# A two-layer encoder trunk: six small moves in the order of a split-precision matmul kernel

## The chip, the cores and the metric

The kernel runs on one core of one Trainium2 chip. The metric is device time in microseconds, from one launch of the program. Three timed runs of the kernel before gave 2052.45, 2053.11 and 2056.63 us; the median is 2053.11 us.

## The reference, cut to what matters

`x` has 256 rows of 2048 numbers in float32. Layer A is a forgetting attention and a feed-forward, then keys and values are made once, then layer B is a chunked attention with its own query projection and a second feed-forward. Everything is computed in float32.

```python
def sq_relu_mlp(h, g, w1, w2):
    a = jax.nn.relu(rms_norm(h, g) @ w1)      # 2048 -> 8192
    return (a * a) @ w2                       # 8192 -> 2048

def reference(x, ...):
    u = rms_norm(h, a_norm_g[l]); proj = u @ a_w_in[l]        # q, k, v and a forget gate per head
    logf = jax.nn.log_sigmoid(fz + a_b_f[l])
    o = forgetting_attention(q, k, v, logf)
    h = h + o.reshape(B, S, D) @ a_w_out[l]
    h = h + sq_relu_mlp(h, mlp_norm_g[0], mlp_w1[0], mlp_w2[0])    # first feed-forward
    kv = rms_norm(h, kv_norm_g) @ kv_w
    q = rms_norm(h, b_norm_g[l]) @ b_w_q[l]                        # query projection
    o = chunked_relbias_attention(q, k_sh, v_sh, b_rel[l])
    h = h + o.reshape(B, S, D) @ b_w_out[l]
    h = h + sq_relu_mlp(h, mlp_norm_g[1], mlp_w1[1], mlp_w2[1])    # second feed-forward
```

## The kernel before, in words

**Units and splits.** All weight matmuls run in a rounded float32 format (fp32r), three passes for one product. A weight *unit* is 128x1024. ScalarE makes `hi`, the rounded copy (L323), VectorE makes `lo = raw - hi` (L324), and TensorE runs hi x x_hi (L592), hi x x_lo (L594) and lo x x_hi (L596), 12 matmuls of 128x512 a unit (or 6, below). There are three `hi` and three `lo` buffers, so the hi of a unit can only be written when the L594 of the unit three before has read its buffer, and its lo when the L596 of that unit has. A split is written into the program two units ahead of its use (`AHEAD`, `fetch`, `top_up`).

**Pairs.** Two blocks of 512 output columns, made for both blocks of 128 rows, form a *pair*, and part of its inner dimension is done by a scheme with seven products in place of eight. A pair has four weight quarters ("11", "12", "21", "22") and four sums of them: T3 = 22 - 12, T2 = T3 + 11, T1 = 12 - 11, T4 = 21 - T2 up to signs. The seven products run in the order 11, T3, T2, T1, then those called 4 (of 21), 5 (of T4, "the fourth sum") and 6 (of 22, "the seventh product"). Products T3, T2, T1 and 22 multiply sums of the activations, called S or Sh, which `sums` makes: four VectorE subtractions (L395 to L398), two ScalarE roundings (L402), two VectorE remainders (L405). In the feed-forward pairs quarters and sums are 2048 columns wide, so each product has two halves of 6 matmuls, and each half is a unit of its own for the ring of three buffers. The rest of the inner dimension goes in *own units*, a4 to a7 and b4 to b7, 12 matmuls each; a is the first block of columns, b the second. The accumulators of a and b are tied by a few instructions on the accumulators: L1007, L1012, L1017 after the second and third product, and L1024 (called V), which adds the saved product `p7`, stands behind the pair's first own unit of a, and must be done ahead of the seventh product and of b's own units. T4 is made by a DMA issued from GpSimd that adds the quarter 21 onto T2's tile in place (`put`, L979).

**Order.** Each engine does its instructions in the order in which the program writes them; a wait at one instruction holds up all behind it on that engine. The table `ORD` holds the order of a pair's own units and last three products (each "F" takes the next of them, in the order that `FO` gives), and the rest of a pair's plan is fixed: four products with the previous pair's last own units b5, b6, b7 between them. Side work stands in a queue of slots, `fill`; `run_fill` takes one slot at each product or own unit. Tables of slot numbers (`T`, `T0H`, `T0K`) say at how many slots after a tile is finished each step of its side work runs.

**Feed-forward.** Each feed-forward runs pairs of the first matrix (hidden tiles) and of the second in turn. The first pair of the first matrix is called "early", the next "second"; then comes "deep0", the first pair of the second matrix, which reads the hidden tiles made by them. A finished hidden tile goes through `turn_hidden`: two VectorE transposes (L440) into `z`; a turn of rows and columns, either through DRAM (L450 writes, L456 reads four pieces) or by sixteen small DMAs that SyncE and GpSimd issue in turn (`hop`, L466); then `take`: Relu on ScalarE (L1045), Square rounded to hi (L1050), Square (L1052), the remainder lo on VectorE (L1056), and for two of a chunk's four tiles the eight instructions of `sums`. The numbers n = 0 to 3 count a chunk's tiles.

**Elsewhere.** The forget gates of layer A (`gates`, `logs`, L876 to L882) run as side work at about 50 to 60 us of the span, while query, key and value products run. The "query" pair, of layer B's projection, follows the first feed-forward's last pair, at about 1035 us.

Of the kernel before, what the change touches and what calls it, by code (L numbers as in the profile page):

```python
# [12 lines left out]
ALU = mybir.AluOpType  # L13
# [18 lines left out]
    "ATB": ((11, 12, 14, 18, 9), (9, 13, 15, 17, 11), (9, 12, 15, 17, 10), (7, 10, 12, 12, 10)),  # L32
# [16 lines left out]
    "OFK": (9, 9, 4, 8, 8, 4),  # L49
# [50 lines left out]
def trunk(ctx: ExitStack, tc: tile.TileContext, xT, xr, gs, hg, bf, wgate, w_in, w_oa, w1a, w1fa, w1sa, w2fa, w2sa,  # L100
# [706 lines left out]
    def begin(u):  # L807
        if u == 0:
            load(2, S, SY)
            S.activation(first, mhalf, AF.Square)  # L810
            SY.dma_start(raw_x[0][:, UA:], xT[:, UA:GH, :])
            load(2)
            load_x(1)
        elif u in (2, 4):
            load_x(u // 2 + 1)
        for j in range(UA):
            x.append(split_x(raw_x[u // 2][:, u % 2 * UA + j], u * UA + j, 0))
        for i, at in enumerate(TABLES["RI"][:3]):
            if u == at:
                rows_in(i)  # L820
        if u >= TABLES["RI"][3]:
            enter(u - TABLES["RI"][3])
# [26 lines left out]
    def gates(x, st):  # L849
# [22 lines left out]
        def logs():  # L872
# [5 lines left out]
            V.tensor_tensor(u, box[0][:H, :T], z, op=ALU.add)  # L878
            V.tensor_tensor(u, u, w, op=ALU.add)
            V.tensor_tensor(u, u, st.R[:H, :], op=ALU.mult)  # L880
            V.tensor_scalar(u, u, bfb, None, op0=ALU.add)
# [15 lines left out]
        def turn_c():  # L897
            pc = ps_o.tile([P, 512], F32, name="pt", tag="po")
            ct["cq"] = const.tile([P, NB, H], F32, name="cq")
            for b in range(NB):  # L900
# [3 lines left out]
        step, spread = steps(logs), steps(st.spread)  # L904
        return [[clear], [], [parts], [lambda: products(range(8))], [lambda: products(range(8, KT))], [spread], [spread],
                [step], [step], [step], [step], [turn_c]]
# [74 lines left out]
    def prepare(p, d):  # L981
# [5 lines left out]
        for name, at in zip(("12", "22", "21", "11", "T3", "T1"), p.units):  # L987
            if d == at and p.deep and name == "T3":
                make(p, "T3", 0)
            elif d == at:  # L990
                (bring if name[0] != "T" else put if p.adds and name == "T1" else make)(p, name)

    def run(plan, open_pair, masks=None, follow=None):
        starts = [i for i, it in enumerate(plan) if it[1:] == (2, 0)] + ([len(plan)] if follow else [])
        for i, (p, q, u) in enumerate(plan):
            hi, lo = ready.popleft()[:2] if q > 1 and ready and not p.deep else fetch()
            if p.ps is None:
# [3 lines left out]
            if q > 1:  # L1001
                assert u != 6 or "V" in p.has, "22 early"
                assert u != 3 or "V" not in p.has, "T1 late"
                form_products(p.ps, hi, lo, p.x, p.fs, u, q == 3, p)
                if u == 1 and q == 2 + p.wide:
                    p.t["P7"] = wk.tile([P, 512], F32, name="p7", tag="wk")
# [13 lines left out]
            else:  # L1020
                assert not p.fast or q == 0 or "V" in p.has, "b early"
                products(p.ps[q], hi, lo, p.x, u, not units and not ready, p.fast)
                if p.fast and (q, u) == (0, p.own):
                    V.tensor_tensor(p.ps[1][1], p.ps[1][0], p.t["P7"], op=ALU.add)  # L1024
                    p.has.add("V")
                for _ in range(1 if masks is None else masks[i]):
# [12 lines left out]
    def mlp(plan, x, Sx, st, last, more=None):  # L1039
# [28 lines left out]
        def turn_hidden(c, n):  # L1068
            zt = []

            def f(b, ps):
# [3 lines left out]
                if b == NB - 1:  # L1075
# [3 lines left out]
                    items = [[] for _ in range(max(at) + 1)]  # L1079
                    for i, d in zip([i for i in at if i >= 0], way + [step] * (len(at) - 2)):  # L1080
                        items[i].append(d)
# [18 lines left out]

    halves_of, owner = {}, {}

# [268 lines left out]
```

## Time and profile before

| | us |
|---|---|
| timed runs, median (lowest, highest) | 2053.11 (2052.45, 2056.63) |
| the profiled execution, its own time | 2058.22 |
| span of that execution, first to last instruction | 2056.4 |
| TensorE matmul busy | 2046.3 |
| VectorE busy | 1784.8 (87%) |
| ScalarE busy | 1403.9 (68%) |
| GpSimd busy | 247.0 (12%) |
| mean granted TensorE clock | 0.999 |
| bytes moved by DMA | 557.78 MB, mean 271 GB/s |

The profile's times are microseconds from the start of the span. A row of the timeline gives the start, the busy time (of all the instructions of a row with a count), engine, source line, operation, tiles and shapes, the count, and in brackets the idle time of that engine just before it and what ended it. PE is the matmul part of TensorE, PEld its weight loads, DVE is VectorE, ACT is ScalarE, POOL is GpSimd, SP is SyncE. Busy times of matmuls overlap their followers a little; the distance between starts is the pace.

### The profile page before, as it was taken

What the parts mean: (1) busy time and instruction counts of PE and PEld (TensorE: products, weight loads), DVE (VectorE), ACT (ScalarE), POOL (GpSimd) and SP (SyncE); (2) the same over time, 40 slices, a digit from 0 to 9 for tenths busy, and PEclk for the clock granted to TensorE, in tenths of its full rate; (3) what the DMA queues carried; (4) which work ended last, traced back from release to release, by engine and by line L of the source; (5) the groups of instructions that cost most, each with busy time, mean ns of one, the idle gap of its engine ahead of it and who ended that gap; (6) DMA issues with size and microseconds to landing.
All of it is one profiled execution on the core that took longest, in us unless ns stands there. A gap on an engine that the chain in (4) does not pass through costs nothing.

```text
span 2056.4 us, 27097 instructions
## 1 busy us (share of the span) xinstructions
PE 2046.3 (100%) x9062; PEld 1688.9 (82%) x9062; DVE 1784.8 (87%) x2065; ACT 1403.9 (68%) x1805; POOL 247.0 (12%) x351
## 2 busy tenths in 40 slices
PE   9999999999999999999999999999999999999999
PEld 8888888878888888888878888888788887888887
DVE  7788898898898899899988778888988997988996
ACT  7766666677677677677778666666766775776764
POOL 1111110021111102101012111001101111111020
PEclk9999999999999999999999999999999999999999
DMA  8898898998888898898889988888989888888984
GB/s 321 262 300 267 268 276 249 298 278 270 283 264 279 271 292 276 254 285 280 244 243 310 279 260 274 251 274 279 288 285 273 272 270 265 257 287 257 300 259 149
DMA packets 175310, 557.78 MB, mean 271 GB/s; under 512 B 40625, under 2 KB 69185, under 8 KB 152641
## 3 DMA queue, kind: packets, MB, share of 16 engines
q1 hardware_dynamic: 154112, 464.99, 64.1%
q0 software_dynamic: 20768, 90.75, 22.6%
q8 instruction: 71, 1.16, 0.2%
q14 instruction: 71, 0.57, 0.1%
q10 hardware_dynamic: 288, 0.30, 0.0%
HBM read 516.07 MB, written 27.29 MB: 264 GB/s over the span
## 4 chain that ended last, share of the span: by engine, by line
PE 92%; DMA 3%; DVE 3%; issue 1%; ACT 1%; SPq 0%; POOL 0%; DVEq 0%; ACTq 0%; POOLq 0%
PE acc L596 22%; PE acc L592 22%; PE acc L594 22%; PE s L596 8%; PE s L592 8%; PE s L594 8%; DVE lo L324 1%; DMA wT<-in_w1fa 1%; DMA wT<-in_w1fb 1%; PE po L729 1%; PE po L766 1%; DMA w<-in_w2fb 1%; DMA q<-turn 0%; DMA R<-turn 0%; PE po L728 0%
## 5 line engine op out<-in xcount | busy, mean ns | idle before, releaser
L324 DVE TENSOR_TENSOR lo<-raw,hi 128x1024 fp32r<-128x1024 f32 (+1 forms) x409 | 494.0, 1212 | 82.2 <-ACT hi L323 78.0
L323 ACT ACTIVATE hi<-raw 128x1024 fp32r<-128x1024 f32 (+1 forms) x409 | 429.2, 1054 | 191.1 <-PE acc L594 127.3
L592 PE MATMUL acc<-hi,act 128*128 128x512 f32 x1774 | 496.4, 393 | 0.9 <-DVE acc L1024 0.6
L596 PE MATMUL acc<-lo,act 128*128 128x512 f32 x1774 | 491.2, 390 | 1.0 <-DVE lo L324 0.8
L594 PE MATMUL acc<-hi,act 128*128 128x512 f32 x1774 | 490.7, 389 | 0.1
L596 PEld LDWEIGHTS acc<-lo,act 128*128 128x128 f32 x1774 | 332.1, 188 | 73.5 <-DVE lo L324 4.7
L594 PEld LDWEIGHTS acc<-hi,act 128*128 128x128 f32 x1774 | 332.8, 188 | 70.4 <-DVE act L421 0.5
L592 PEld LDWEIGHTS acc<-hi,act 128*128 128x128 f32 x1774 | 331.4, 188 | 70.5 <-ACT hi L323 1.8
L323 ACT ACTIVATE hi<-w 128x1024 fp32r<-128x1024 f32 x254 | 266.7, 1058 | 125.8 <-PE acc L594 82.2
L324 DVE TENSOR_TENSOR lo<-wT,hi 128x1024 fp32r<-128x1024 f32 x220 | 267.2, 1221 | 68.6 <-ACT hi L323 64.7
L324 DVE TENSOR_TENSOR lo<-w,hi 128x1024 fp32r<-128x1024 f32 x254 | 305.4, 1217 | 17.2 <-ACT hi L323 15.0
L323 ACT ACTIVATE hi<-wT 128x1024 fp32r<-128x1024 f32 x220 | 231.9, 1060 | 106.3 <-PE acc L594 58.2
L592 PE MATMUL s<-hi,act 128*128 128x512 f32 x530 | 146.4, 391 | 0.0
L596 PE MATMUL s<-lo,act 128*128 128x512 f32 x530 | 145.2, 389 | 0.0
L594 PE MATMUL s<-hi,act 128*128 128x512 f32 x530 | 144.8, 388 | 0.0
L466 POOL DMA_DIRECT2D q<-z x192 | 95.7, 510 | 256.3 <-DVE z L440 210.9
L596 PEld LDWEIGHTS s<-lo,act 128*128 128x128 f32 x530 | 99.0, 188 | 21.4 <-DVE lo L324 1.2
L594 PEld LDWEIGHTS s<-hi,act 128*128 128x128 f32 x530 | 99.4, 188 | 20.7
L592 PEld LDWEIGHTS s<-hi,act 128*128 128x128 f32 x530 | 98.9, 188 | 20.5 <-ACT hi L323 0.4
L592 PE MATMUL s<-hi,S 128*128 128x512 f32 x288 | 89.5, 392 | 0.0
L594 PE MATMUL s<-hi,S 128*128 128x512 f32 x288 | 88.7, 389 | 0.0
L596 PE MATMUL s<-lo,S 128*128 128x512 f32 x288 | 88.7, 389 | 0.0
(217 smaller groups left out, 2291.5 us busy)
## 6 DMA issues: line engine op xcount, KB each, us to landing
raw<-in_w_in SPq DMA_DIRECT2D x75, 512.0 KB, 5.9
w<-in_w2fa SPq DMA_DIRECT2D x32, 1024.0 KB, 6.1
w<-in_w2fb SPq DMA_DIRECT2D x32, 1024.0 KB, 6.3
w<-in_w1fa SPq DMA_DIRECT2D x27, 1024.0 KB, 7.2
w<-in_w1fb SPq DMA_DIRECT2D x27, 1024.0 KB, 7.4
raw<-in_w2sa SPq DMA_DIRECT2D x52, 512.0 KB, 7.6
raw<-in_w2sb SPq DMA_DIRECT2D x50, 512.0 KB, 7.1
raw<-in_w_kv SPq DMA_DIRECT2D x48, 512.0 KB, 5.0
```

The lines of the kernel that those rows point to most:

```text
L323: S.activation(hi[:, c], raw[:, c], AF.Copy)
L324: V.tensor_tensor(lo[:, c], raw[:, c], hi[:, c].bitcast(F32), op=ALU.subtract)
L466: (G if i % 2 else SY).dma_start(dst[32 * j : 32 * j + 32, i * n : (i + 1) * n], z[32 * i : 32 * i + 32, j * n : (j + 1) * n])
L592: TE.matmul(ps[:, cols], xh, cut(hi, j), start=first, stop=False, **kw)
L594: TE.matmul(ps[:, cols], xl, cut(hi, j), start=False, stop=False, **kw)
L596: TE.matmul(ps[:, cols], xh, cut(lo, j), start=False, stop=last, **kw)
L729: TE.matmul(s[:, P : 3 * P], q[:, a, P:T], k[:, a], start=True, stop=True)
L766: TE.matmul(po[:, :T], v[:, 0, a * P : (a + 1) * P], pT[:, :2], start=True, stop=False)
```

## The change

Six moves, with no arithmetic added or left out.

1. The first weight unit is loaded in two halves. The first half goes from ScalarE's DMA queue to SyncE's, the second half the other way.
2. Forget gates: a `yield` is put behind the two additions L878 and L879, and their step (two ScalarE copies L876, L877 and these additions) now runs one slot earlier, in the slot of the spread of the row statistics. The three instructions behind (L880 to L882) stay where they were.
3. Query pair: V (L1024, which becomes L995) is written ahead of the fetch of own unit b2, and so ahead of the split that this fetch issues.
4. "second" pair, in both feed-forwards: `FO` from "456" to "465" and `ORD` from "a4 F F a5 a6 a7 F b4" to "a4 F F a5 F a6 a7 b4". TensorE's order from a4 on was a4, 21, T4, a5, a6, a7, 22, b4 and is a4, 21, 22, a5, T4, a6, a7, b4.
5. First feed-forward only: the four subtractions of `sums` for the first hidden tile (n = 0) are put in a queue `later` and run directly behind the next product's first half.
6. With 4, own unit a7 is the seventh item from a4 on where it was the sixth. The side work of a's hidden tile is counted in slots from the end of a7, so each of its steps comes one item later against the next pair. The tables of slots are unchanged.

```diff
-    "FO": {"second": "456", ..., "query": "465"},
+    "FO": {"second": "456", ..., "query": "465", "second": "465"},
...
-    "ORD": {"second": "a4 F F a5 a6 a7 F b4", ...
+    "ORD": {"second": "a4 F F a5 F a6 a7 b4", ...
...
-            load(2, S, SY)
+            load(2, SY, S)
...
             V.tensor_tensor(u, u, w, op=ALU.add)
+            yield
             V.tensor_tensor(u, u, st.R[:H, :], op=ALU.mult)
...
-        return [[clear], [], [parts], [lambda: products(range(8))], [lambda: products(range(8, KT))], [spread], [spread],
+        return [[clear], [], [parts], [lambda: products(range(8))], [lambda: products(range(8, KT))], [spread], [spread, step],
                 [step], [step], [step], [step], [turn_c]]
...
+    def join_v(p):
+        V.tensor_tensor(p.ps[1][1], p.ps[1][0], p.t["P7"], op=ALU.add)
+        p.has.add("V")
...
         for i, (p, q, u) in enumerate(plan):
+            early_v = p.order == "query" and (q, u) == (0, p.own)
+            if early_v:
+                join_v(p)
             hi, lo = ready.popleft()[:2] if q > 1 and ready and not p.deep else fetch()
...
                 form_products(p.ps, hi, lo, p.x, p.fs, u, q == 3, p)
+                while later and q == 2:
+                    later.popleft()()
...
-                if p.fast and (q, u) == (0, p.own):
-                    V.tensor_tensor(p.ps[1][1], p.ps[1][0], p.t["P7"], op=ALU.add)
-                    p.has.add("V")
+                if p.fast and (q, u) == (0, p.own) and not early_v:
+                    join_v(p)
...
-                    for i, d in zip([i for i in at if i >= 0], way + [step] * (len(at) - 2)):
+                    todo = way + [step] * (len(at) - 2)
+                    if more and (c, n) == (0, 0):
+                        todo[5] = lambda: later.append(step)
+                    for i, d in zip([i for i in at if i >= 0], todo):
                         items[i].append(d)
```

**First place: ScalarE in the "second" pair of the first feed-forward.** The tile `w21` is the quarter 21, `w22` the quarter 22, `wT3` the tile in which T4 stands, `raw` and `zraw` are own units, `q` is the turned hidden tile, `sum` and `Sh` belong to `sums`. Before, from the second half of product 21 on:

```order
L323 ACTIVATE hi_4051<-w21_3755 128x1024
L323 ACTIVATE hi_4079<-wT3_3801 128x1024
L323 ACTIVATE hi_4089<-wT3_3801 128x1024
L402 ACTIVATE Sh_4068<-sum_4069 128x512
L402 ACTIVATE Sh_4068<-sum_4070 128x512
L323 ACTIVATE hi_4103<-raw_3863 128x1024
L323 ACTIVATE hi_4115<-zraw_3923 128x1024
L323 ACTIVATE hi_4127<-raw_3966 128x1024
L1045 ACTIVATE q_4004<-q_4004 128x1024
L323 ACTIVATE hi_4149<-w22_3718 128x1024
L1050 ACTIVATE act_4146<-q_4004 128x1024
```

And now:

```order
L323 ACTIVATE hi_4051<-w21_3755 128x1024
L323 ACTIVATE hi_4072<-w22_3718 128x1024
L323 ACTIVATE hi_4089<-w22_3718 128x1024
L402 ACTIVATE Sh_4082<-sum_4083 128x512
L402 ACTIVATE Sh_4082<-sum_4084 128x512
L323 ACTIVATE hi_4103<-raw_3863 128x1024
L323 ACTIVATE hi_4115<-wT3_3801 128x1024
L323 ACTIVATE hi_4125<-wT3_3801 128x1024
L1054 ACTIVATE q_4004<-q_4004 128x1024
L323 ACTIVATE hi_4145<-zraw_3923 128x1024
L323 ACTIVATE hi_4157<-raw_3966 128x1024
L1059 ACTIVATE act_4142<-q_4004 128x1024
```

Product 22 has taken T4's place behind 21, T4 stands behind own unit a5 (`raw_3863`), and the Relu of the hidden tile (L1045, now L1054) stands ahead of the hi of a6 (`zraw_3923`) and a7 (`raw_3966`), where it stood behind them.

**Second place: ScalarE in "deep0", the next pair, from the first half of T1 to product 21.** Here `w12` is the tile of T1, `raw` own unit a4 and `w21` product 21; the last line of `take` before the remainder is L1052, now L1061. Before:

```order
L323 ACTIVATE hi_4346<-w12_4007 128x1024
L1045 ACTIVATE q_4187<-q_4187 128x1024
L323 ACTIVATE hi_4359<-w12_4007 128x1024
L1050 ACTIVATE act_4358<-q_4187 128x1024
L1052 ACTIVATE q_4187<-q_4187 128x1024
L1037 ACTIVATE acc_4248<-acc_4251 128x512
L323 ACTIVATE hi_4383<-raw_4194 128x1024
L323 ACTIVATE hi_4395<-w21_4240 128x1024
L323 ACTIVATE hi_4405<-w21_4240 128x1024
```

And now:

```order
L323 ACTIVATE hi_4346<-w12_4007 128x1024
L323 ACTIVATE hi_4357<-w12_4007 128x1024
L1054 ACTIVATE q_4215<-q_4215 128x1024
L1046 ACTIVATE acc_4248<-acc_4251 128x512
L323 ACTIVATE hi_4380<-raw_4174 128x1024
L323 ACTIVATE hi_4392<-w21_4240 128x1024
L1059 ACTIVATE act_4374<-q_4215 128x1024
L1061 ACTIVATE q_4215<-q_4215 128x1024
L323 ACTIVATE hi_4405<-w21_4240 128x1024
```

The two squares (L1050, L1052; now L1059, L1061) stood ahead of the hi of a4 and of 21's first half and stand behind both. `act_4358`, now `act_4374`, is what own unit a4 multiplies. The second feed-forward shows the same move.

**Third place: VectorE in the query pair.** `w21` is product 21, `raw_8997` (and the same tile now) own unit b2, `h0`, `h1` the residual rows. Before:

```order
L324 TENSOR_TENSOR lo_9139<-w21_8989,hi_9138 128x1024
L324 TENSOR_TENSOR lo_9143<-raw_8997,hi_9142 128x1024
L1024 TENSOR_TENSOR acc_9021<-acc_9020,p7_9062 128x512
L440 STREAM_TRANSPOSE z_9161<-h0_90 128x4x4x32
```

And now:

```order
L324 TENSOR_TENSOR lo_9139<-w21_8989,hi_9138 128x1024
L995 TENSOR_TENSOR acc_9021<-acc_9020,p7_9062 128x512
L324 TENSOR_TENSOR lo_9144<-raw_8997,hi_9143 128x1024
L440 STREAM_TRANSPOSE z_9161<-h0_90 128x4x4x32
```

V and the lo of b2 have changed places.

More of the change, by code (lines that the diff above doesn't have):

```diff
@@ L1099, in mlp @@
         run(plan, open_pair, None, plan_k[0][0] if more else None)
-    halves_of, owner = {}, {}
+    halves_of, owner, later = {}, {}, deque()
     def sub(tag):
```

4 rows, old and new, of the table TABLES are left out of this document.

## The prediction

> **What bounds the kernel now.** I read the page first, then TensorE's waits, then the timeline at each edited place.
>
> ```profile
> span 2056.4 us, 27097 instructions
> PE 92%; DMA 3%; DVE 3%; issue 1%; ACT 1%; SPq 0%; POOL 0%; DVEq 0%; ACTq 0%; POOLq 0%
> PE acc L592 <- DVE acc L1012: 2.1, 1, 2.1
> PE acc L596 <- DVE lo L324: 0.8, 2, 0.6
> PE acc L592 <- DVE acc L1024: 0.6, 1, 0.6
> ```
>
> The chain that ended last is TensorE for 92%. No matmul is added or removed, so the change can win only the moments at which TensorE stands still, and lose by new ones. The list of its waits (us in all, how often, the longest) is short: 0.6 us behind V (L1024) and 0.8 us behind remainders (L324) are what the edits aim at; the largest, 2.1 us, is in the second feed-forward and none of them touches it. The list leaves out what a late start costs the matmuls behind it, so below I measure stalls as distance between starts against the undisturbed pace. That pace is seen below: a pass of 2 matmuls takes 0.45 (432.44 to 432.89), one of 4 takes 0.91 (470.03 to 470.94).
>
> The profiled execution took 2058.2 us, 1.8 around the span and 5.1 over the median of 2053.11. All sums are changes to its own stretches, and I add them to the median. I call 0.2%, 4.1 us, the least that a measurement can tell from no change.
>
> **Start, first weight halves.**
>
> ```profile
> raw<-in_w_in ACTq DMA_DIRECT2D x1, 256.0 KB, 4.5
> raw<-in_w_in SPq DMA_DIRECT2D x1, 256.0 KB, 4.2
> 18.25 1.06 ACT L323 ACTIVATE hi<-raw 128x1024 fp32r<-128x1024 f32 x1 [1.02 <-DMA raw<-in_w_in]
> 20.48 0.88 DVE L383 SCALAR_TENSOR_TENSOR act<-xin,gsb,act 128x256 fp32r<-128x256 f32 x2
> 21.06 1.32 PE L594 MATMUL acc<-hi,act 128*128 128x512 f32 x4
> ```
>
> SyncE's half lands 4.2 us after issue, ScalarE's 4.5, and the first hi needs the first half: the swap can start it up to 0.3 us earlier. But at 21.06 TensorE again waits inside a pass (1.32 busy where 1.07 is usual) for the activations that VectorE ends at 20.48 + 0.88 = 21.36, and ahead of these stands a hi that waited 1.02 us for a weight. What is gained at 5 us is waited for there. I take 0; bounds -0.3 and 0.
>
> **Gates.**
>
> ```profile
> 53.50 1.23 DVE L324 TENSOR_TENSOR lo<-wT,hi 128x1024 fp32r<-128x1024 f32 x1 [2.53 <-ACT hi L323]
> 54.67 0.41 DVE L878 TENSOR_TENSOR gu<-pg,gz 16x256 f32<-16x256 f32 x1
> 56.73 1.21 DVE L324 TENSOR_TENSOR lo<-raw,hi 128x1024 fp32r<-128x1024 f32 x1
> 57.99 1.20 PE L596 MATMUL acc<-lo,act 128*128 128x512 f32 x4 [0.19 <-DVE lo L324]
> 59.03 0.62 PE L592 MATMUL s<-hi,S 128*128 128x512 f32 x2
> ```
>
> The five gate instructions run between the two remainders, and the second remainder ends at 57.94, when TensorE has already waited. Its L594 began at 56.73, so L596 was due at 57.64 and the next row at 58.55: 0.48 us late. Two of the five (0.45 apart, so 0.9) now run in the 2.53 us in which VectorE stands idle before 53.50. The second remainder then ends near 57.04, ahead of 57.64. The term is -0.48, with 0 as the other bound, if the two additions wait for their ScalarE copies and push the first remainder instead.
>
> **Query pair.**
>
> ```profile
> 1040.89 0.69 DVE L1024 TENSOR_TENSOR acc<-acc,p 128x512 f32<-128x512 f32 x1
> 1040.51 0.61 PE L596 MATMUL acc<-lo,act 128*128 128x512 f32 x2
> 1041.73 1.16 PE L592 MATMUL acc<-hi,act 128*128 128x512 f32 x4 [0.61 <-DVE acc L1024]
> ```
>
> Due at 1040.51 + 0.45 = 1040.96, b2 began at 1041.73, since V stood behind b2's own remainder. Now V comes one remainder (1.1 to 1.2) earlier, near 1039.7, and the remainder ends near 1041.6. It is needed by b2's third pass, two passes of 0.91 after 1040.96, near 1042.8, so its delay lies under the first two. The term is -0.77. If V were held by something that the order puts before it, the least would be 0.
>
> **"second" pair, first feed-forward.**
>
> ```profile
> 432.44 0.61 PE L592 MATMUL acc<-hi,act 128*128 128x512 f32 x2
> 432.89 0.61 PE L594 MATMUL acc<-hi,act 128*128 128x512 f32 x2
> 434.14 0.73 PE L596 MATMUL acc<-lo,act 128*128 128x512 f32 x2 [0.63 <-DVE lo L324]
> 438.62 1.07 PE L596 MATMUL acc<-lo,act 128*128 128x512 f32 x4
> 431.40 0.41 DVE L395 TENSOR_TENSOR sum<-q 128x256 f32<-128x256 f32 x1
> 432.87 1.22 DVE L324 TENSOR_TENSOR lo<-wT,hi 128x1024 fp32r<-128x1024 f32 x1
> 434.66 1.23 DVE L324 TENSOR_TENSOR lo<-wT,hi 128x1024 fp32r<-128x1024 f32 x1 [0.58 <-ACT hi L323]
> 439.77 1.06 ACT L1045 ACTIVATE q<-q 128x1024 f32<-128x1024 f32 x1 [1.26 <-DMA w<-in_w2fa]
> 458.44 0.73 PE L596 MATMUL acc<-lo,Sh 128*128 128x512 f32 x2
> ```
>
> From 432.44 to 438.62 stand six passes of 2 and two of 4, 4.5 us at full pace, in 6.18: T4's late sum and the `sums` ahead of its remainder cost 1.65 us. Another 0.24 is lost at 458.44. That 1.9 is the most the edit can win here. Now I lay the new order over these durations. VectorE does the remainder of 22's first half at 431.4, then the four subtractions, and 22's second remainder from 434.0 to 435.2; TensorE wants it at 434.7: 0.5 late. ScalarE then reaches the Relu of the hidden tile, which began at 439.77 after 1.26 us of waiting. The row names a weight's DMA; what the Relu reads is `q`, so I take it that the last of the sixteen small DMAs held it. The hi's of the next two units used to be done by then; now those of a6 and a7 stand behind it. The hi of a6 ends near 441.9, TensorE wants a6 near 441.2: 0.7 later. From here VectorE, which has one gap of 0.58 to give, runs without idle time up to the next pair, and it carries the end: the wait that was 0.24 at 458.44 becomes one at the pair's last halves too. By hand this comes out at +0.6 for the stretch against before. Bounds: -1.9, every wait gone, and +1.3, the Relu's wait and the subtractions in full. I take +0.6, since VectorE's rows there leave no gap for a gain.
>
> **"second" pair, second feed-forward.**
>
> ```profile
> 1450.09 0.73 PE L596 MATMUL acc<-lo,act 128*128 128x512 f32 x2
> 1454.35 0.85 PE L592 MATMUL acc<-hi,act 128*128 128x512 f32 x3
> ```
>
> Seven passes of 2, 3.17 at pace, stand in 4.26: 1.1 to win. Here the subtractions aren't deferred. VectorE's gap for T4's hi goes, a like one opens at the remainder of b4, whose hi stands behind Relu and square: I take -0.1, bounds -1.1 and +0.5.
>
> **"deep0", own unit a4, both feed-forwards.** Here the forecast is decided.
>
> ```profile
> 465.84 1.05 ACT L1050 ACTIVATE act<-q 128x1024 fp32r<-128x1024 f32 x1
> 466.92 1.06 ACT L1052 ACTIVATE q<-q 128x1024 f32<-128x1024 f32 x1
> 469.35 1.99 ACT L323 ACTIVATE hi<-w 128x1024 fp32r<-128x1024 f32 x2
> 468.01 1.23 DVE L1056 TENSOR_TENSOR act<-q,act 128x1024 fp32r<-128x1024 f32 x1 [0.82 <-ACT q L1052]
> 468.22 0.61 PE L596 MATMUL acc<-lo,Sh 128*128 128x512 f32 x2
> 470.03 1.07 PE L592 MATMUL acc<-hi,act 128*128 128x512 f32 x4
> 470.94 1.07 PE L594 MATMUL acc<-hi,act 128*128 128x512 f32 x4
> 1485.56 1.23 DVE L1056 TENSOR_TENSOR act<-q,act 128x1024 fp32r<-128x1024 f32 x1 [0.82 <-ACT q L1052]
> ```
>
> Own unit a4 multiplies the tile that L1050 and L1056 finish. Before, the squares ran at 465.84 and 466.92 and the remainder at 468.01, two microseconds ahead of 470.03. Now both squares stand behind the hi of a4 and of 21's first half (second place in the change). The latter overwrites the buffer of T1's first half, so it can't start until T1's L594 is through, at 468.22. From there: hi 0.95, the square 1.05 (done at 470.2), the second square 1.06 (471.3), the remainder 1.23: 472.5. TensorE wants the hi for 470.03 and the remainder for its second pass at 470.94. It waits some 0.2, and then to 472.5: 1.6 in all, and with the slower pass after a stall (0.73 for 0.61 at 434.14) 1.7. The second feed-forward has the same rows (the remainder at 1485.56 with the same 0.82 idle ahead): +1.7 again. In the first the turned tile could land too late for the Relu's new place as well: it lost its spare of some microseconds when a7 moved one item back. For that 0 to 1.2; I take 0.3, nearer to 0, as the turned tile is on the chip well ahead in before. If the squares get through in time, because the buffer comes free earlier than I read it, the term is 0.
>
> **The sum.** 0 - 0.48 - 0.77 + 0.6 - 0.1 + 1.7 + 0.3 + 1.7 = +2.95 us, so 2053.1 + 2.95 = 2056.1: slower by 0.14%, which no measurement tells from no change. The unknowns of the two "second" pairs and the late tile give this case 2054.5 to 2058.
>
> **Rival 1: the clock.** A stall can cost more than itself.
>
> ```profile
> 1731.90 0.70 PE L592 MATMUL acc<-hi,Sh 128*128 128x512 f32 x2 [2.05 <-DVE acc L1012]
> 1732.00:1736.00 4.00, 4.00 (x12) 3.14 (x13) 4.00 (x5) 1.76 (x3) 0.00 (x0) 0.63 0.98 247
> 434.00:440.00 6.00, 5.81 (x23) 4.02 (x24) 5.42 (x7) 4.74 (x7) 0.24 (x1) 1.00 0.98 378
> ```
>
> (In a window's row the number before the DMA share is the granted clock.) After the wait of 2.05 us the clock was 0.63 of full over 4 us, (1 - 0.63) x 4 = 1.5 us more. In 434 to 440, with some 1.6 us lost in pieces, it stayed 1.00. The new stall at a4, 0.2 and 1.4 us close together, lies between. If it trips the clock once or twice, the sum is +4.4 to +5.9, 2057.6 to 2059.0. It decides from a stall somewhere between 1.6 and 2.05 us on. The Trainium skill ("TensorE: Matmul & The Clock Gate", section "What's actually happening") says that the half rate comes after an idle window of about 3.4 us, in windows that run freely; by it a stall of 1.7 us would cost no clock and the sum would stay +2.95. The row at 1731.90 differs, as 2.05 us were enough there, and the measurement decides.
>
> **Rival 2: the waits just go.** If the squares are in time and the order of "second" does what it says, what is left is -0.48 - 0.77 and between -0.9 (VectorE's gap of 0.58 in the one and some tenths in the other) and -3.0 (1.9 and 1.1) for the pairs: -2.2 to -4.3, 2048.9 to 2051.0. For it speaks that 1.9 and 1.1 us of stall do stand there; against it that VectorE has no idle time to give from 435 to 458, and the place of the squares.
>
> **Rival 3: half of it.** Only one feed-forward stalls at a4, or the first's "second" pair comes out even: +0.3 to +1.5, 2053.4 to 2054.6. The two feed-forwards' rows at a4 are so alike that I give it little.
>
> **How the numbers follow.** The forecast 48% (a sixth of it over +4.1), the clock 20% (all but a tenth of it over +4.1), the waits gone 20% (half of it under -4.1: with the start's -0.3 it reaches -4.6), half of it 12%. Slower by over 0.2% is 0.08 + 0.18 = 0.26, faster 0.10, the same 0.64. The range leaves out the far half of rival 2 and the last tenth of the clock's: 2050.4 to 2059.4. The likeliest case's own is 2054.5 to 2058.
>
> **What would show it.** Start: TensorE's first product up to 0.3 earlier, and the same end at 22.2. Gates: no wait at L596 near 58. Query: b2 0.45 behind 21's last pass. "second": no wait of a T4 remainder, but ScalarE idle at the Relu ahead of a6's hi, and a TensorE wait there. "deep0": waits of a4 for the activations of 1.5 us and more, in both feed-forwards, with the granted clock beside them. I am wrong if the squares of the third hidden tile end before 470 in that stretch, if TensorE's waits of 432 to 436 simply vanish without others in 440 to 459, or if the 2.05 us at 1731.90 moves with the change.

## The result, and the profile after

The changed kernel took 2057.15 us (median of 12 runs, 2056.15 to 2061.62) beside 2052.07 us for the kernel before (12 runs, 2050.67 to 2056.63). The ratio is 1.0024, 95% interval 1.0017 to 1.0032: 4.9 us slower, between 3.5 and 6.6. The forecast was +2.95 us, or 2056.1 us. In absolute time it is only 1 us off, but that is partly luck: it was added to the median of three runs, 2053.11, which is 1 us above the median of the twelve.

The profiled execution of the changed kernel has the shorter span all the same, 2054.7 against 2056.4 us. That is no contradiction: TensorE's waits of the kernel before included one of 2.1 us at 1731 us, with 1.5 us of lowered clock behind it, and a second profile of the kernel before has no such wait and a span of 2050.0. One profile of each would have given the wrong sign. The page's span and TensorE's waits (waiter, awaited; us in all, how often, the longest) after, those of 0.4 us and more without the one of 1.0 at the program's start:

```profile
span 2054.7 us, 27099 instructions
PE acc L594 <- DVE act L1065: 2.3, 2, 1.2
PE acc L592 <- ACT act L1059: 1.3, 2, 1.0
PE s L596 <- DVE lo L324: 0.4, 1, 0.4
PE acc L596 <- DVE lo L324: 0.4, 1, 0.4
```

The two waits at the head are new. L1059 is the first square and L1065 the remainder of the third hidden tile (L1050 and L1056 before), so these are own unit a4 of deep0, two times, once for the hi and once for the remainder of its activations. The query pair's wait for V is gone. The timeline at that place, first feed-forward (TensorE, ScalarE, VectorE), then second (TensorE):

```profile
467.09 0.62 PE L596 MATMUL acc<-lo,Sh 128*128 128x512 f32 x2
468.71 1.20 PE L592 MATMUL acc<-hi,act 128*128 128x512 f32 x4 [1.01 <-ACT act L1059]
471.06 1.19 PE L594 MATMUL acc<-hi,act 128*128 128x512 f32 x4 [1.15 <-DVE act L1065]
472.09 1.09 PE L596 MATMUL acc<-lo,act 128*128 128x512 f32 x4
464.25 1.06 ACT L1054 ACTIVATE q<-q 128x1024 f32<-128x1024 f32 x1 [1.34 <-DMA q<-turn]
466.67 1.04 ACT L323 ACTIVATE hi<-w 128x1024 fp32r<-128x1024 f32 x1
467.62 1.04 ACT L1059 ACTIVATE act<-q 128x1024 fp32r<-128x1024 f32 x1
468.69 1.06 ACT L1061 ACTIVATE q<-q 128x1024 f32<-128x1024 f32 x1
469.78 1.22 DVE L1065 TENSOR_TENSOR act<-q,act 128x1024 fp32r<-128x1024 f32 x1 [0.62 <-ACT q L1061]
1487.65 1.19 PE L592 MATMUL acc<-hi,act 128*128 128x512 f32 x4 [0.28 <-ACT act L1059]
1490.01 1.21 PE L594 MATMUL acc<-hi,act 128*128 128x512 f32 x4 [1.16 <-DVE act L1065]
```

At full pace a4 would have begun at 467.54 and its third pass at 469.35; the third pass began at 472.09, 2.7 us late. The order is the one of the second place in the change: hi of product 21 at 466.67, then the squares, then the remainder, which ends at 471.0, when the second pass starts. In the first feed-forward the Relu also waits 1.34 us for the turned tile.

The places of the other edits, after: the gates, the query pair, the "second" pair.

```profile
56.84 1.07 PE L594 MATMUL acc<-hi,act 128*128 128x512 f32 x4
57.75 1.07 PE L596 MATMUL acc<-lo,act 128*128 128x512 f32 x4
1040.90 0.62 PE L596 MATMUL acc<-lo,act 128*128 128x512 f32 x2
1041.35 1.07 PE L592 MATMUL acc<-hi,act 128*128 128x512 f32 x4
433.26 0.73 PE L596 MATMUL s<-lo,S 128*128 128x512 f32 x2 [0.40 <-DVE lo L324]
436.72 1.06 ACT L1054 ACTIVATE q<-q 128x1024 f32<-128x1024 f32 x1 [1.14 <-issue]
437.69 1.04 ACT L323 ACTIVATE hi<-zraw 128x1024 fp32r<-128x1024 f32 x1
430.64 0.50 POOL L466 DMA_DIRECT2D q<-z  x1 [2.76 <-DMA wT<-in_w1fa]
```

The last row stood so in the kernel before:

```profile
433.75 0.50 POOL L466 DMA_DIRECT2D q<-z  x1 [2.69 <-DMA q<-z]
```

Gates: L596 follows L594 by 0.91, the full pace; the wait is gone. Query: b2 begins 0.45 after 21's last pass, the wait is gone. "second": T4's wait has become one of 0.40 at 22's second remainder, behind the four subtractions, as laid out. The Relu ahead of a6's hi did idle ScalarE, but it ran at 436.72, and a6's hi was done at 438.7, before TensorE wanted it (439.36). GpSimd's last small DMA of that hidden tile was issued at 430.64, against 433.75 before, so the tile came earlier.

Both kernels were profiled a second time, and these runs took 2051.77 and 2057.02 us, 5.25 apart, about as the medians are (5.08). The next table gives how much later the changed kernel reaches the same matmul at the end of each stretch than at its beginning, from the starts of the matmuls of both pairs of profiles:

| stretch | forecast | first pair of profiles | second pair |
|---|---|---|---|
| start, to 50 us | 0 | +0.2 | -0.5 |
| gates | -0.48 | -0.5 | -0.5 |
| to 404 us | 0 | -1.6 | 0.0 |
| "second" pair, first feed-forward | +0.6 | -0.5 | +0.15 |
| deep0's a4, first | +2.0 | +2.7 | +2.4 |
| to 1035 us | 0 | +0.1 | -0.4 |
| query pair | -0.77 | -0.85 | -0.7 |
| to 1440 us | 0 | +0.1 | +1.2 |
| "second" pair, second feed-forward | -0.1 | 0.0 | +0.9 |
| deep0's a4, second | +1.7 | +2.0 | +2.0 |
| to the end | 0 | -3.3 | +0.5 |
| sum | +2.95 | -1.7 | +5.0 |

The steps that I costed are much alike in both pairs, apart from the "second" pairs. What makes the sums differ so much are the stretches that no edit touches, and there chance waits, mostly on transfers: the largest are those at 283 us and at 1731 us in the first profile of the kernel before.

### The profile page after: what moved, and what is told of

Same layout as the page of the kernel before. It is cut to its first block, busy times and chain, and to the rows that moved or that the text cites. A ratio compares the mean times of both kernels' runs of the same rounds, so it can differ in the third digit from the quotient of the medians.

```text
span 2054.7 us, 27099 instructions
## 1 busy us (share of the span) xinstructions
PE 2044.2 (99%) x9062; PEld 1688.5 (82%) x9062; DVE 1784.1 (87%) x2065; ACT 1404.4 (68%) x1805; POOL 245.8 (12%) x351
## 3 DMA queue, kind: packets, MB, share of 16 engines
q8 instruction: 71, 1.16, 0.2%
## 4 chain that ended last, share of the span: by engine, by line
PE 94%; DMA 2%; DVE 2%; ACT 1%; issue 1%; POOL 0%; SPq 0%; DVEq 0%; ACTq 0%; POOLq 0%
PE acc L594 22%; PE acc L596 22%; PE acc L592 22%; PE s L596 9%; PE s L592 9%; PE s L594 9%; DVE lo L324 1%; DMA wT<-in_w1fa 1%; ACT hi L323 1%; PE po L729 1%; PE po L766 1%; DMA q<-turn 0%; PE po L767 0%; PE po L728 0%; DMA turn<-z 0%
## 5 line engine op out<-in xcount | busy, mean ns | idle before, releaser
L594 PE MATMUL acc<-hi,act 128*128 128x512 f32 x1774 | 490.9, 390 | 2.3 <-DVE act L1065 2.3
L596 PE MATMUL acc<-lo,act 128*128 128x512 f32 x1774 | 490.9, 390 | 0.6 <-DVE lo L324 0.4
L594 PEld LDWEIGHTS acc<-hi,act 128*128 128x128 f32 x1774 | 332.8, 188 | 73.1 <-DVE act L1065 3.2
L596 PEld LDWEIGHTS acc<-lo,act 128*128 128x128 f32 x1774 | 332.5, 188 | 71.7 <-DVE lo L324 2.6
L596 PE MATMUL s<-lo,act 128*128 128x512 f32 x530 | 145.2, 389 | 0.1
L594 PE MATMUL s<-hi,act 128*128 128x512 f32 x530 | 144.8, 388 | 0.0
L596 PEld LDWEIGHTS s<-lo,act 128*128 128x128 f32 x530 | 99.0, 188 | 21.6 <-DVE lo L324 1.4
L594 PEld LDWEIGHTS s<-hi,act 128*128 128x128 f32 x530 | 99.4, 188 | 20.6
L596 PE MATMUL s<-lo,S 128*128 128x512 f32 x288 | 88.9, 390 | 0.4 <-DVE lo L324 0.4
L594 PE MATMUL s<-hi,S 128*128 128x512 f32 x288 | 88.7, 389 | 0.0
```

The source lines that it names most:

```text
L594: TE.matmul(ps[:, cols], xl, cut(hi, j), start=False, stop=False, **kw)
L596: TE.matmul(ps[:, cols], xh, cut(lo, j), start=False, stop=last, **kw)
```

## The experiments

Theory 1, mine: a4's wait for the squares is the loss, and a stall costs itself. Theory 2: the loss comes from transfers elsewhere, which any shift of issue times lengthens. Theory 3: the stalls at a4 lower the clock, and that is the rest of the loss. Each is told apart by what moves with a4.

### The change without the new order

```diff
-    "FO": {"second": "456", ..., "query": "465", "second": "465"},
+    "FO": {"second": "456", ..., "query": "465"},
-    "ORD": {"second": "a4 F F a5 F a6 a7 b4", ...
+    "ORD": {"second": "a4 F F a5 a6 a7 F b4", ...
```

> The change without its new order of the second pair (the order of a4, 21, T4, a5, a6, a7, 22, b4 is restored); all other edits stay. Theory 1 (the squares behind product 21's hi make deep0's a4 wait): no wait of a4 near 470 and 1488 us, T4's waits near 434 and 1451 are back (some 1 us in each feed-forward, less in the first, where the sums are deferred), the gates' and the query's gains of 0.5 and 0.8 us stay: 1 to 2 us faster than before. Theory 2 (the loss comes from late transfers elsewhere, for instance the wait at 1731 us, which any shift of the issue times can lengthen): slower than before by 2 us or more, with the loss in waits on transfers.

Measured: 2052.19 us (11 runs) beside 2052.67 (24 runs); ratio 0.9992, interval 0.9983 to 1.0001. No wait of a4 for its activations is left. Run once more:

> The change without the new order of the second pair once more, for more runs of the best candidate: edits 1 to 3 and 5. Theory 1: 1.2 us from edits 2 and 3 and 0.3 to 0.5 from a shorter wait of T4 in the first feed-forward: 1.5 us faster than before, a ratio of 0.9993.

Measured: 2052.30 us (12 runs) beside 2053.12 (26 runs); ratio 0.9997, interval 0.9988 to 1.0006. So the loss sits in the new order, and theory 2 is out as the main cause. The gain of 1.5 us that was expected of the rest is not shown: both intervals hold no change, and the second holds +0.06%.

### The new order alone, on the kernel before

The same two rows of the tables, put into the kernel before.

> The kernel before with only the new order of the second pair in both feed-forwards. Theory 1: a4 of deep0 waits about 2.7 us in the first feed-forward and 2.0 in the second, T4's waits are shorter by 1 us in the first at most and 0.6 in the second, gates and query as before: 4 to 6 us slower than before, more than the whole change's loss of 5 less 1.3. Theory 2: no more than 2 us slower.

Measured: 2058.15 us (7 runs); ratio 1.0026, interval 1.0015 to 1.0036, 5.3 us slower.

```profile
PE acc L594 <- DVE act L1056: 2.3, 2, 1.2
PE acc L592 <- ACT act L1050: 1.1, 2, 0.6
PE acc L592 <- DVE acc L1024: 0.6, 1, 0.6
```

These are three of its TensorE waits: a4's two, and V's, which this kernel keeps. The order alone makes the whole loss. Its profile has another wait, of 1.84 us for one remainder in the second feed-forward's "second" pair (VectorE, then TensorE):

```profile
1462.41 1.23 DVE L969 TENSOR_TENSOR wT<-w,w 128x1024 f32<-128x1024 f32 x1 [3.10 <-DMA w<-in_w2fb]
1464.82 1.20 PE L596 MATMUL acc<-lo,act 128*128 128x512 f32 x4 [1.84 <-DVE lo L324]
```

L969 (L970 in the change) makes the next pair's first weight sum, and here it waited 3.10 us for a weight to land. The new order puts it ahead of the remainders of a6 and a7, the old one behind both, so a late weight now holds up TensorE. In both profiles of the change the sum waited 0.5 us at most and cost nothing that shows; in that of the later Relu, below, it waited 1.91 and TensorE 0.65. This is a second price of the new order, paid in some executions only.

### Squares one slot earlier

```diff
-    "T0H": (..., (0, 4, 6, 7, 7, 7), ...),
+    "T0H": (..., (0, 3, 5, 6, 6, 6), ...),
-    "T0K": (..., (1, 3, 6, 7, 7, 7), ...),
+    "T0K": (..., (0, 2, 5, 6, 6, 6), ...),
```

> The whole change with the side work of the second pair's a tile (columns of the turn, Relu, squares, remainder) one slot earlier, by two rows of the tables of slots. Theory 1: in the second feed-forward the wait of a4 near 1488 (2.0 us) goes; in the first the turned tile lands only near 464, so that a wait of 1 us at most is left of 2.7. Together 3 to 4 us less than the whole change, so 1 to 2 us over before. Theory 2: as slow as the whole change.

Measured: 2055.59 us (11 runs); ratio 1.0014, interval 1.0005 to 1.0022. By the ratios 2 us of the change's 4.9 are gone, less than the 3 to 4 expected. ScalarE and TensorE in the first feed-forward, and TensorE in the second:

```profile
463.46 1.06 ACT L1054 ACTIVATE q<-q 128x1024 f32<-128x1024 f32 x1 [2.26 <-DMA q<-turn]
465.37 1.04 ACT L1059 ACTIVATE act<-q 128x1024 fp32r<-128x1024 f32 x1
467.93 1.04 ACT L323 ACTIVATE hi<-raw 128x1024 fp32r<-128x1024 f32 x1
469.02 1.20 PE L592 MATMUL acc<-hi,act 128*128 128x512 f32 x4 [1.50 <-ACT hi L323]
1487.46 1.19 PE L592 MATMUL acc<-hi,act 128*128 128x512 f32 x4 [0.28 <-ACT hi L323]
```

The Relu, written earlier, just waits longer (2.26 us) for the turned tile, and now a4's own weight split stands behind the squares, so a4 waits 1.50 us for its hi. In the first feed-forward the turned tile is too late for either order; in the second the wait falls from 0.28 and 1.16 to 0.28 (0.9 us late by the starts, in place of 2.0).

### Own unit a4 behind product 21

```diff
+    "ORD": {..., "deep0f": "F a4 F F b4 a5 a6 a7"},        # and "deep0f": "465" in FO
-                add(None, w2f, w2s, i, WIDE2, "deep%d" % q, ...
+                add(None, w2f, w2s, i, WIDE2, "deep%d" % q + "f" * (i == 0), ...
-            early_v = p.order == "query" and (q, u) == (0, p.own)
+            early_v = p.order in ("query", "deep0f") and (q, u) == (0, p.own)
+                    if (c, n) == (0, 2):
+                        todo[3] = lambda: later.append(step)
-    (0, 4, 6, 7, 7, 7) in T0H, (1, 3, 6, 7, 7, 7) in T0K
+    (0, 4, 6, 6, 7, 7) in T0H, (1, 3, 6, 6, 7, 7) in T0K
```

> The whole change, and in deep0 of each feed-forward own unit a4 stands behind product 21 in place of ahead of it (21, a4, 22, T4, b4), with V ahead of a4's split and the first of the two squares of the third hidden tile between the hi's of 21's halves. Nothing else moves; the turned tile lands as late as in the change. Theory 1 (only the order of the squares against a4 costs): a4 starts 2.7 us later and finds its activations, its waits near 469 and 1488 us (2.7 and 2.0 us) fall to under 0.5 each, so 3 to 5 us less than the whole change, 0 to 2 us less than before. Theory 2 (whatever makes the change slower is not tied to a4): as slow as the whole change. Theory 3 (the clock gives the rest of the loss): the same as theory 1, and the times scatter as narrowly as before's.

Measured: 2053.42 us (12 runs) beside 2053.91 (18 runs); ratio 1.0000, interval 0.9992 to 1.0009. The change's 1.0024 is undone while everything else of it stays.

```profile
469.73 0.73 PE L596 MATMUL acc<-lo,act 128*128 128x512 f32 x2
470.36 1.20 PE L592 MATMUL acc<-hi,act 128*128 128x512 f32 x4
471.40 1.08 PE L594 MATMUL acc<-hi,act 128*128 128x512 f32 x4
473.83 0.70 PE L592 MATMUL acc<-hi,Sh 128*128 128x512 f32 x2 [0.44 <-DVE acc L995]
```

Own unit a4 now starts at 470.36, 0.18 late, and finds its activations; what is left is a wait of 0.44 for V, which stands behind 22's first remainder there. In the second feed-forward no wait is left at that place: a4 starts at 1488.20, 0.45 after the pass ahead of it. This is the run that settles the cause: the matmuls, the transfers and the order of the "second" pair are those of the change, and a4 comes later. V and the first square moved with it (the diff), so what it settles is that the loss hangs on the order of a4 and its squares, and not on a4's place by itself. It doesn't beat the kernel before.

### The Relu later still

```diff
-    (0, 4, 6, 7, 7, 7) in T0H, (1, 3, 6, 7, 7, 7) in T0K
+    (0, 4, 7, 7, 7, 7) in T0H, (1, 3, 7, 7, 7, 7) in T0K
```

> The whole change with the Relu of the third hidden tile one slot later still, behind the hi of product 21, so that a4 of deep0 waits for three ScalarE steps in place of two. Theory 1 (a stall costs itself): a4's waits grow by 1.0 us each, to 3.0 to 3.7 us; 2 us slower than the whole change, granted clock 1.00 in the stretches behind them. Theory 3 (stalls of this size trip the clock): the clock behind a4 falls to 0.6 to 0.8 over 4 us in at least one of the two places, 3.5 to 5 us slower than the whole change.

Measured: 2061.54 us (5 runs) beside 2053.91; ratio 1.0039, interval 1.0025 to 1.0052. That is 3 us more than the change by the ratios, between the two expectations. The profile shows why: a4's waits are the same in both feed-forwards, and only one lowered the clock. TensorE at both places, and the windows (us, busy times of the engines, granted clock, DMA share, GB/s) around the second:

```profile
468.19 1.20 PE L592 MATMUL acc<-hi,act 128*128 128x512 f32 x4 [1.37 <-ACT act L1059]
470.54 1.20 PE L594 MATMUL acc<-hi,act 128*128 128x512 f32 x4 [1.16 <-DVE act L1065]
471.57 1.08 PE L596 MATMUL acc<-lo,act 128*128 128x512 f32 x4
1491.16 1.19 PE L592 MATMUL acc<-hi,act 128*128 128x512 f32 x4 [1.38 <-ACT act L1059]
1493.51 2.07 PE L594 MATMUL acc<-hi,act 128*128 128x512 f32 x4 [1.16 <-DVE act L1065]
1495.38 1.78 PE L596 MATMUL acc<-lo,act 128*128 128x512 f32 x4
...
1488.00:1492.00 4.00, 2.62 (x12) 1.80 (x11) 2.30 (x2) 3.93 (x4) 3.51 (x7) 1.00 1.03 245
1492.00:1496.00 4.00, 2.84 (x8) 2.00 (x7) 2.97 (x3) 1.52 (x3) 0.16 (x1) 0.68 0.98 248
1496.00:1500.00 4.00, 4.00 (x18) 3.21 (x17) 2.00 (x2) 2.23 (x3) 0.34 (x1) 0.89 0.45 122
```

In the second, passes of 4 take 1.78 to 2.07 in place of 1.07. By the windows the loss is (1 - 0.68) x 4 + (1 - 0.89) x 4 = 1.7 us; by the starts of the matmuls it is 1.5, as the two passes took 3.49 us here and 1.95 in the first feed-forward. So theory 3 is a real price of stalls of this size, paid in one of two places in this execution. All five timed runs show some of it: their mean granted clocks are 0.997 to 0.999, where the 18 runs of the kernel before beside them all have 1.000. By the rows the waits grew by 0.4 us in the first feed-forward, where the late tile had already cost most of the Relu's place, and by 1.1 in the second; 1.0 each was expected. With the clock that makes some 3 us, as measured, but that it closes so well is luck: the interval of the ratio is 5.5 us wide, and this profile has the 0.65 us of the late weight besides.

### Second profiles of both kernels

> The changed kernel once more, for a second profile. Theory 1: the two waits of a4 are there with 2.3 to 2.8 and 1.9 to 2.1 us, and waits on transfers elsewhere differ from the first profile. Theory 3: a granted clock under 1.00 behind one of them.

> The kernel before once more, for a second profile. Theory 1: T4's waits near 434 (1.6 us with slow passes) and 1451 (1.1), the gates' near 58 (0.5) and the query pair's near 1041 (0.8) stand again; the wait of 2 us at 1731 is a matter of the execution and may be gone.

Measured: 2057.02 and 2051.77 us, one run each. TensorE's waits of the change again (the two rows of a4), and in the kernel before the place of T4 in the first feed-forward and the row that had waited 2.05 us:

```profile
PE acc L594 <- DVE act L1065: 2.3, 2, 1.2
PE acc L592 <- ACT act L1059: 1.0, 2, 0.7
```

```profile
432.47 0.61 PE L594 MATMUL acc<-hi,act 128*128 128x512 f32 x2
433.71 0.72 PE L596 MATMUL acc<-lo,act 128*128 128x512 f32 x2 [0.63 <-DVE lo L324]
437.49 1.07 PE L596 MATMUL acc<-lo,act 128*128 128x512 f32 x4
1448.39 0.73 PE L596 MATMUL acc<-lo,act 128*128 128x512 f32 x2
1452.08 1.07 PE L592 MATMUL acc<-hi,act 128*128 128x512 f32 x4
1727.19 0.62 PE L592 MATMUL acc<-hi,Sh 128*128 128x512 f32 x2
```

The clock stayed at 1.00 behind a4 in the change, in its second profile as in its first, of which the two windows are:

```profile
468.00:472.00 4.00, 2.14 (x8) 1.48 (x9) 3.38 (x4) 2.66 (x3) 1.80 (x4) 1.00 1.03 255
1488.00:1492.00 4.00, 2.84 (x13) 1.99 (x12) 2.97 (x3) 2.38 (x3) 1.35 (x3) 1.00 0.96 247
```

In the second profile of the kernel before, T4 costs less than in the first: 432.47 to 437.49 is 5.02 us for what needs 4.08 (five passes of 2 at 0.453, two of 4 at 0.907), 0.9 in place of 1.65, and 1448.39 to 1452.08 is 3.69 for seven passes of 2, 0.5 in place of 1.1. The wait at 1731 is absent.

### The deferred subtractions, and the small edits alone

```diff
-                    if more and (c, n) == (0, 0):
+                    if False:
```

> The whole change without the deferred subtractions of the first hidden tile (edit 5): the four stand where they stood before, ahead of 22's first remainder. Theory 1: the wait near 433 grows from 0.56 to about 0.8 us and passes after it slow down, so 0.3 to 0.6 us slower than the whole change (4.5 to 6 over before), which timing can hardly tell; a4's two waits unchanged. If the deferral itself did harm, for instance by moving the second rounding, it is 1 us or more faster than the whole change.

Measured: 2057.02 us (8 runs) beside 2053.12; ratio 1.0019, interval 1.0010 to 1.0029, the same as the whole change within what timing can tell. The wait at 22's second remainder is 0.6 in place of 0.4, as expected. This profile also has what the prediction laid out for a6: the Relu begins at 438.48 after 2.81 us of idle ScalarE, the hi of a6 behind it, and a6 starts 0.2 us late, at 440.54.

The same line, and the old order of the "second" pair, so that edits 1 to 3 are left:

> Edits 1 to 3 alone (first halves' queues, gate additions, V of the query pair). Theory 1: the waits near 58 (0.5 with the slow pass) and 1041 (0.75) go, nothing else moves: 1.2 us faster than before, within what timing can tell. T4's waits as before.

Measured: 2051.50 us (11 runs) beside 2053.12; ratio 0.9995, interval 0.9987 to 1.0004: 1.0 us faster by its middle, where 1.2 was expected, but no change is inside. The waits of gates and query pair are gone from its list of waits.

### T4 last: a miss

```diff
-    "ORD": {"second": "a4 F F a5 F a6 a7 b4", ...
+    "ORD": {"second": "a4 F F a5 a6 a7 F b4", ...         # FO stays "465"
+    "W2F0": (6, 5, 1, 5, 2, 1),                           # deep0 of chunk 0: T3 and T1 two units later each
```

> The whole change, but the second pair's own units stay where they were before and only T4 and 22 change places (a4, 21, 22, a5, a6, a7, T4, b4); T3 of the next pair is then made later, as it needs T4's tile. Own unit a7 is the sixth item again, so the squares of its hidden tile stand ahead of deep0's a4 as before. Theory 1: no wait of a4 near 470 and 1488 us, none of T4's waits, gates' and query's gains kept: 2 to 4 us faster than before, if the later T3 costs nothing (it is made right ahead of its split, which may cost up to 1 us in each feed-forward). Theory 2: as slow as the whole change.

Measured: 2059.49 us (6 runs); ratio 1.0029, interval 1.0018 to 1.0041. Here T4's product comes after its accumulator has been read out, so T4 is missing from the a tile of the "second" pair: T4 belongs to a's accumulators, 22 to b's. What was expected could not happen:

```profile
PE acc L593 <- DVE z L441: 3.2, 2, 1.9
```

(The row at the head of its waits. Its lines stand one lower in the code: L593 is a first pass, L441 the transposes of a finished tile.) TensorE waits for the transposes that read a's accumulators before T4 may write them. It says nothing on theory 1 and is no way to a better order: T4 must stand ahead of a7, so a place behind a5 needs a7 one item later.

## Why the prediction was right or wrong

**deep0's a4: right, and short by 0.7 to 1.0 us in all.** It was forecast at +1.7 and +1.7, and +0.3 for a late turned tile: +3.7. Measured are 2.4 to 2.7 and 2.0, together 4.4 to 4.7, with the order, the waits and the rows as told. The mis-sized terms: each stall cost 2.0 in place of 1.7, as the second feed-forward shows, where the Relu didn't wait for its tile. There the hi of product 21 started at 1485.59, 1.6 us ahead of a4's due time of 1487.20, where the prediction had 1.8, and the remainder ended 4.4 us after that start in place of 4.3. The late tile in the first feed-forward cost 0.4 to 0.7 in place of 0.3 (the Relu waits 1.34 us for it in the first profile and 1.02 in the second). One sign of being wrong was met by the letter: the squares ended at 469.75, ahead of 470. But TensorE was 2.5 us earlier there, with a4 due at 467.54 where it had begun at 470.03, so the sign should have been set against a4 and not against a time. The wait at 1731.90, another sign, did shrink to 0.3 in the change, but it is gone from the kernel before's second profile as well.

**Gates and query pair: right.** -0.5 and -0.7 to -0.85 against -0.48 and -0.77.

**Start: not settled.** The first product begins at 6.01 us in the change, where it began at 6.38 and 6.12. By 50 us small waits had taken it back in one pair of profiles (+0.2), and 0.5 us had stayed in the other. Both lie outside the bounds of -0.3 and 0, and two profiles of each can't tell this from chance.

**"second" pair, first feed-forward: the number held, the way didn't.** Forecast +0.6, measured -0.5 and +0.15. 22's late remainder came as laid out; the Relu that was to hold a6 by 0.7 us did not. The step that failed is taking the time of the last small DMA over from before: TensorE was 2 us earlier at that place already (the stretches ahead of it), and the DMA was issued at 430.64, 3.1 us earlier than before. The last microsecond was the first profile's own: in the second profiles GpSimd's last issue is at 431.75 before and 430.49 after, 1.3 us apart, with TensorE 1.0 earlier. So 433.75 was a late case, and where the tile is late again (the change without the deferred subtractions) a6 is late too, by 0.2 us.

**"second" pair, second feed-forward: the baseline failed.** Forecast -0.1, measured 0.0 against the profile that I had, and +0.9 against the second. The 1.65 and 1.1 us that stood as T4's cost were those of one execution; in the other they were 0.9 and 0.5. There was less to win than the first profile showed, while the new order's own wait (0.5 us at 1470, where the transposes of a's tile, one item later, stand between the subtractions and the remainder that TensorE wants) is in both profiles of the change and in neither of the kernel before (0.35 in one of three other profiles with the old order). The 0.2 at 1476 that they also have stands in the kernel before too, at 1475.99 in its first profile. The new order's late weight, 1.84 us in one other execution, comes on top at times.

**Rival 1, the clock: not in the two profiles of the change, but likely in some of its runs.** Its two profiles, four places in all, show no wait of a4 that lowers the clock, nor does the profile of the order alone, so the clock isn't the main loss. But the timed runs have a mean granted clock on record, all but the twelve of the kernel before beside the change. It is 0.999 in the two profiled executions in which the clock fell once while matmuls ran (the first of the kernel before, the later Relu), and 1.000 in the other eleven. It is 0.999 in 4 of the change's 12 runs, its three slowest among them, and with its second profile, the order alone and the change without the deferral in 9 of 28. In the kernels in which a4 doesn't wait for its squares (the kernel before, the three runs of the old order and the one of a4 behind 21) it is 0.999 in 8 of 114. (Left out: squares one slot earlier, 1 of 11, and T4 last, 2 of 6.) The mean doesn't say where the clock fell, and a fall behind the last matmul counts into it as well, so this is a share and no proof; as an estimate from these counts, a quarter of the runs pay 1.5 us, some 0.4 us on average. With 0.4 and 1.1 us more of waiting (the Relu later) one place of two paid 1.5 to 1.7 us. My boundary "between 1.6 and 2.05 us" was not it, as two waits of 1.38 and 1.16 us with one pass of four matmuls between them sufficed once, and 1.37 and 1.16 didn't in the other place. The Trainium skill ("TensorE: Matmul & The Clock Gate", section "What's actually happening") has windows that run freely of the kernel; that agrees with one of two like places being hit. That an idle window of some 3.4 us is needed does not: TensorE was busy for 2.62 us of the 4 up to 1492, and for 2.84 of the 4 in which the clock fell, with a pass of 1.19 us between the two waits.

**Rival 2, the waits just go: no.** T4's waits did go, but a4's came. **Rival 3: no.** Both feed-forwards stall.

**The sum and the chances.** Over the stretches that I costed, the start among them, the table adds up to +3.05 in the first pair of profiles and +3.75 in the second, beside a forecast of +2.95: errors of up to 1.1 us at a term, mostly against each other. The runs say +4.9, and the interval begins at 3.5. What is over lies in stretches that no edit touches: +1.3 us in the second pair of profiles, most of it in small waits between 1041 and 1440 us, and -4.7 in the first, the chance waits of the kernel before. The small waits between 1041 and 1440 us don't come from the new order or a4's waits: from the matmul at 1043.83 to the one at 1438.35 the second profile of the kernel before takes 394.5 us, its first 395.0, the change 395.1 and 395.8, and the three profiles with the old order and the small edits 394.8, 395.7 and 396.2. So there the second profile of the kernel before was a fast case. What makes up the rest of the 4.9 stays open; the clock (some 0.4 us on average) and the late weight of the second feed-forward may be parts of it that the costed terms didn't hold. So the mechanism gave the sign, and I gave 0.64 to no change and 0.26 to slower; at +4.9 it is slower by a little more than the 4.1 us that I called measurable.

## What to carry to other kernels

When a unit of work is moved by one item, follow everything that is counted from its end, not only the unit: here the gain at T4 was looked for in the "second" pair, and most of the price was paid 35 us later, where squares on ScalarE had slid behind a weight split that waits for TensorE. The order of an engine's instructions shows such a slide before anything runs. And a wait that depends on a transfer is worth what it costs in several executions, not in the one profiled: T4's waits were 2.75 us in one and 1.5 in the other, and a single profile of each kernel made the change 1.7 us faster where it is 4.9 slower.

## What the runs showed of the hardware

The clock of TensorE fell to 0.68 over 4 us after two waits of 1.38 and 1.16 us with one pass of four matmuls (1.19 us) between them, and in the same execution stayed at 1.00 after 1.37 and 1.16 us in the same arrangement. The lowered clock lasts some 3.5 us (passes of 4 at 2.07 and 1.78 us, the next pass of 2 at 0.63 again) and cost 1.5 us by the starts of the matmuls, 1.7 by the granted clock. In the kernel before it fell after a single wait of 2.05 us, and there too cost 1.5 us.
